# Two changes around an attention block's output projection: a written-out order for its tail, and the affine factors of the layer normalisation moved behind the transposition

## The chip, the cores and the metric

The kernel runs on one core of one Trainium2 chip. The metric is the device time of one execution in microseconds (us), shown as the median of three runs. TensorE (PE in the profile) multiplies matrices, VectorE (DVE), ScalarE (ACT) and GpSimd (POOL) do elementwise work, and SyncE (SP) issues the DMA transfers. Each engine works through its own queue of instructions in order and waits on semaphores for the others.

## The reference

The reference computes two layers of a decoder trunk for one sequence of 1024 tokens of width 1024, in float32. Layer 0 mixes tokens by dilated window attention, layer 1 by a gated linear recurrence (HGRN2). Each mixer is followed by a feed-forward block of width 4096 with a squared ReLU. Each of these four parts is added to its input and normalised:

```python
def layer_norm(x, g, b):
    xf = x.astype(F32)
    mu = jnp.mean(xf, axis=-1, keepdims=True)
    var = jnp.mean(jnp.square(xf - mu), axis=-1, keepdims=True)
    return ((xf - mu) * lax.rsqrt(var + LN_EPS) * g.astype(F32) + b.astype(F32)).astype(x.dtype)
...
for i in range(DEPTH):
    x = layer_norm(ALPHA * x + mixer(x), ln_mix_g[i], ln_mix_b[i])
    x = layer_norm(ALPHA * x + squared_relu_mlp(x, w_up[i], w_down[i]), ln_ffn_g[i], ln_ffn_b[i])
```

The loop is shortened. The affine factors g and b of a normalisation are vectors along the 1024 features.

The attention has three head groups with (window, dilation) = (128, 1), (512, 4) and (2048, 16). For each group it projects to q, k and v, rotates q and k by position (rotary embedding), computes softmax attention within the window, and at the end mixes the three groups' outputs per position and head, weighted by their softmax denominators. The mixed output, 1024 wide, is projected by W_out.

## The kernel before

**Precision.** Every matmul operand is split into a high and a low part (names end in h and l), and a product is three matmuls: high by high, low by high, high by low. The function `split` (L136 to L138) makes the parts: one instruction on ScalarE copies the high part (L137), one on VectorE subtracts it from the raw value (L138). In the large products the kernel uses Strassen's scheme with seven products for eight blocks, hence the many sums and differences of blocks (wc, wa, T1 to T4, S1 to S4).

**Stages.** By the trace: attention products and attention until 973 us, the projection by W_out with the last attention units until about 1118, the first feed-forward (up, then down) until about 1755, HGRN and its projection until 2250, the second feed-forward until the end.

**Attention.** `attention()` runs over `seq`, a list of product slots; in each slot TensorE computes one 512-wide product of twelve matmuls (L666 to L668). Three slots make the q, k and v of a unit of heads and a group. When the products of a unit are there, its attention is entered in a dictionary `fill` at slots given by tables: `ROPES` (rotary: `rope`, L465 to L474, four DMA issues that swap halves into a tile `rot`, a multiply by cos, L472, a multiply by sin, L473, an addition, L474), `OFFS` (the core: `qk` with the scores s, L500, the masked maximum, L511, the exponential, L514, `ptr` with the transposition ppt, L524, and `pv` with the output o, L539), `STATS` (the transposition mpt of the softmax statistics, L564) and `MIX` (the mix of the three groups: small [16, 128] instructions mn and ml, L592 to L605, the split of the weights into fh and fl, L609 and L611, six DMA issues that lay them out as rows, frow, L616, matmuls fb that spread them over the heads, L626, and the multiplications with the outputs og, L627 to L630). Steps due in a slot are issued behind its product.

TensorE and VectorE are kept in program order up to the last slot (`order`, an `in_order` block). Behind it a scheduler orders the instructions by its own costs and the program's priorities. The steps of the last two units, (7,1) and (7,0), and of the units whose slots lie past the end, come back from `attention()` as the list `lists`.

**Projection tail.** `outproj_ln()` (used for W_out of attention, `Out` with mixer 0, and of HGRN, mixer 1) computes z = ALPHA * x + o W_out by tiles of 128 tokens t and halves of 512 columns dm, over eight blocks k of 128 rows of W_out. For the attention k = 0 to 5 are ready first (`NKA`), so `stage_a` computes their part of some tiles, three tiles (0,0), (1,0), (2,0) together, then (0,1), (1,1), (2,1), (3,0), (3,1) one by one, and `tick()` issues the steps of `lists` between them, in equal shares of the ticks (a tick is three matmuls, L183 to L185). The z part is added by L933. Three blocks k (`PREA`) have their W_out and o split ahead, in the last slots of the attention. Behind the mix, `fin(t)` computes the rest of each tile, normalises it with `ln_math` and stores it to `x1d`; `tr(t)` transposes it (lnpt, L223) and splits it for the feed-forward (class `Fast`, which also keeps raw copies and forms the sums for Strassen's scheme, fs, L297 to L305).

**Layer normalisation.** `ln_math` (L193 to L214) does it in place on a [128, 1024] tile z:

```python
nc.vector.scalar_tensor_tensor(z, z, mv[:, 0:1], gB, op0=ALU.subtract, op1=ALU.mult)
...
act(z, z, AF.Copy, scale=w[:, 3:4])
nc.gpsimd.tensor_add(z, z, bB)
```

Statistics on VectorE (L196, L198), the subtraction of the mean and the multiplication with gB (g spread over the partitions) on VectorE (L199), the reciprocal root by Ln and Exp on ScalarE and a correction step on VectorE (L204 to L206), the scaling on ScalarE (L213), the addition of bB on GpSimd (L214). Only the last normalisation, with a store to the output, goes another way.

**Feed-forward.** `ffn()` computes up and down products in Strassen's scheme. In the down phase a function `after(n)` appends the closing work to a list `todo`, of which one entry is issued behind each step: residual loads, sums, `norm_of` (the normalisation and its store to `x3d`, L1296), `tr`/`ln_tr` (the transposition lnpt and the split of f0nh and f0nl, L233 and L234, directly out of the transposition's PSUM bank). No engine is kept in program order in the down phase. The loads of d (hidden activations, L1181) and their split d3s are on SP, ScalarE and VectorE next to that. The gates of HGRN begin directly behind.

Of the kernel before, what the change touches and what calls it, by code (L numbers as in the profile page):

```python
# [32 lines left out]
NSLOT = 50  # L33
NPRE = 2
PREA = 3
# [22 lines left out]
ROPES0 = ((-5, -2, -1, 2), (-4, 0, 1, 4))  # L58
# [4 lines left out]
def trunk_kernel(  # L63
# [15 lines left out]
    w_down: bass.AP,  # L79
    cos_t: bass.AP,  # L80
# [10 lines left out]
    wp = ctx.enter_context(tc.tile_pool(name="wp", bufs=3))  # L91
# [42 lines left out]
    nc.gpsimd.memset(one, 1.0)  # L134

# [57 lines left out]
    def ln_math(z, gB, bB, store=None):  # L193
# [5 lines left out]
        nc.vector.scalar_tensor_tensor(z, z, mv[:, 0:1], gB, op0=ALU.subtract, op1=ALU.mult)  # L199
        w = small([P, 4], "lnw")  # L200
# [6 lines left out]
        if store is not None:  # L207
            for i in range(2):
                c = slice(i * 512, i * 512 + 512)
                nc.vector.scalar_tensor_tensor(z[:, c], z[:, c], w[:, 3:4], bB[:, c], op0=ALU.mult, op1=ALU.add)  # L210
                nc.sync.dma_start(store[:, c], z[:, c])
            return
        act(z, z, AF.Copy, scale=w[:, 3:4])  # L213
        nc.gpsimd.tensor_add(z, z, bB)  # L214
# [21 lines left out]
    def ln_tr(t, z, xs):  # L236
        x_ = xs[t // 4]
        c = slice((t % 4) * P, (t % 4) * P + P)
        for j, pt in enumerate(z_tr(z)):
            put(x_.hi[2 * j:2 * j + 2], x_.lo[2 * j:2 * j + 2], pt, c)  # L240

    class Fast:


        def __init__(self, name):
            self.name, self.parts, self.raw, self.seen = name, {}, {}, []
# [18 lines left out]
        def add(self, t, z):  # L271
# [3 lines left out]
            v, g = nc.vector, nc.gpsimd  # L275
# [5 lines left out]
            def put_(n, src, eng=None):  # L281
                put(*self.tiles(n), src, c, eng)

            if half == 0:
                put_("11", p0)
                put_("21", p1)
            else:
                put_("22", p1)
            if first:
                a, b = ("11", "21") if half == 0 else ("12", "22")  # L290
                act(self.keep(a, t), p0, AF.Copy)
                act(self.keep(b, t), p1, AF.Copy)
                return
            t1, t2, t3, t4 = (scratch(n) for n in (1, 2, 3, 4))
            if half == 1:
                w12 = scratch(0)
                act(w12, p0, AF.Copy)  # L297
                v.tensor_sub(t3, p1, w12)
                g.tensor_sub(t1, w12, self.keep("11", t))
                put_("T3", t3)  # L300
                v.tensor_sub(t2, p1, t1)
                put_("T1", t1)
                g.tensor_sub(t4, self.keep("21", t), t2)
            else:
                b22 = self.keep("22", t)  # L305
                v.tensor_sub(t1, self.keep("12", t), p0)
                g.tensor_sub(t3, b22, self.keep("12", t))
                g.tensor_sub(t2, b22, t1)
                put_("T1", t1)
                v.tensor_sub(t4, p1, t2)  # L310
                put_("T3", t3)
# [10 lines left out]
    def attention(pre, hc):  # L322
# [124 lines left out]
        def constants():  # L447
            nc.sync.dma_start(cosT, cos_t)
            nc.sync.dma_start(sinT, sin_t)
            nc.sync.dma_start(mask, masks)  # L450

# [24 lines left out]
        def pieces(pr, g, qT, kT, vT, og, sS):  # L476
# [53 lines left out]
            def pv(b):  # L530
                if b % 4 == 0:
                    st["o"] = bank("o", "o")
# [19 lines left out]

            return [
# [152 lines left out]
        def unit_work(gi, a, base):  # L706
# [12 lines left out]
            def begin():  # L719
                ogs[pr][g] = U("og")  # L720
                p = pieces(pr, g, res.pop((a, 0)), res.pop((a, 1)), ep.pop((gi, 2, a)), ogs[pr][g], sS)
# [18 lines left out]
        order.__enter__()  # L740
        load_x("21", 0, (L, R))
# [19 lines left out]
        for n in range(len(seq)):  # L761
            gi, i, j = seq[n]
            load_w(n + LOADW)
# [12 lines left out]
            if n == len(seq) - 2 * PREA - 3:  # L776
                early = pre(oN)
            if n >= len(seq) - 2 * PREA - 1:
# [10 lines left out]
            if n % 21 == 14:  # L789
# [3 lines left out]
                for a in range(2):  # L793
# [14 lines left out]
                    for k, f in zip(MIX[a], mix):  # L808
                        at(base + k, f)
                if last:  # L810
                    for a in range(2):
                        for k, f in list(zip(ROPES0[a], tail[a][0])):
                            if k < -1:
# [4 lines left out]
        done = [f for n in sorted(fill) for f in fill[n]]  # L818
        mine = [[ra[0]], [rb[0], rb[1]], [ra[1]], [ca[0], rb[2]], [ca[1]], [cb[0]], [ca[2]], [cb[1]], [ca[3]], [cb[2]],
                [ca[4]] + sa, [cb[3]], [ca[5]], [cb[4]] + sb_, [cb[5]], mx[:1], mx[1:3], mx[3:5], [],  # L820
                mx[5:7], mx[7:10], mx[10:]]
        lists = [done[k:k + 1] + (mine[k] if k < len(mine) else []) for k in range(max(len(done), len(mine)))]
        return oN, lists


    class Out:
# [11 lines left out]
        def pre_steps(self, oN):  # L838
            for k in range(PREA):
                self.load(k, oN, 0)  # L840
                raw = U("wor")
                self.w[k] = (None, None, raw)
                nc.sync.dma_start(raw[:, :512], self.w_dram[k][:, :512])

            def steps():
                for k in range(PREA):
                    raw = self.w[k][2]
                    hi, lo = U("woh", F32R), U("wol", F32R)
                    self.w[k] = hi, lo, raw
                    split(raw[:, :512], hi[:, :512], lo[:, :512])  # L850
                    yield
                    self.split_k(k, 0)
                    yield

            return steps()
# [30 lines left out]
    def outproj_ln(pr, oN, fill, resid, gB_ap, bB_ap, keep):  # L886
# [864 lines left out]
```

## Time and profile before

| what | value |
| --- | --- |
| median of three runs | 2857.04 us (2854.59 to 2858.03) |
| the profiled execution's own time | 2856.82 us |
| its span, first to last instruction | 2854.6 us |
| mean granted TensorE clock | 0.995 |
| busy: TensorE, VectorE, ScalarE, GpSimd | 2789.4, 2053.8, 1448.4, 122.6 us |
| transfers | 485.25 MB, 170 GB/s |

A row of the profile names a line of the kernel, an engine, an operation and "out<-in" by the program's tile names without numbers. In a timeline the first two columns are start and duration in us. In the view of waits a row says which engine at which line waited for whom, then the total in us, how often, and the longest. Windows give, for a stretch of time, the busy time of each engine and the clock that was granted to TensorE (1.00 is full speed). A matmul of 512 columns is listed with 0.39 us, but the next one starts 0.227 us behind it; so the pace is read from starts, not from durations.

### The profile page before, as it was taken

To read this page: it belongs to the slowest core of one execution; us is meant where nothing else is said; L and a number is where in the kernel's file an instruction comes from. 1 tells how busy PE (TensorE), PEld (TensorE's weight loads), DVE (VectorE), ACT (ScalarE), POOL (GpSimd) and SP (SyncE) were. 2 spreads that over 40 slices of the span, in tenths; PEclk is the share of its full clock that TensorE was granted. 3 is DMA by queue.
4 is the path that set the end of the run, shared out by engine and by line. 5 is a ranking of instruction groups with operands and counts; after the bars stand their busy time and mean duration, and the time that the engine had idled before them with its cause. 6 is when DMAs were issued, how large, how long until landed. Compare 5 with 4: busy or idle time off the path is not lost.

```text
span 2854.6 us, 39893 instructions
## 1 busy us (share of the span) xinstructions
PE 2789.4 (98%) x14152; PEld 2235.3 (78%) x14152; DVE 2053.8 (72%) x3830; ACT 1448.4 (51%) x3105; POOL 122.6 (4%) x67
## 2 busy tenths in 40 slices
PE   8999999999999989999999999999999999999998
PEld 6777777777777767888878887778787788878887
DVE  7768777776887767786686875555667787678677
ACT  5555555655555555544454444554553645454433
POOL 0000000000000003000000011111102200000000
PEclk9999999999999999999999999999999999999999
DMA  7766665666667523464584843101131455475654
GB/s 291 249 201 193 190 197 171 215 206 204 198 198 222 154 77 133 156 220 156 173 303 126 275 142 104 38 30 60 51 120 71 159 202 174 155 268 189 223 176 132
DMA packets 204935, 485.25 MB, mean 170 GB/s; under 512 B 29376, under 2 KB 43712, under 8 KB 204736
## 3 DMA queue, kind: packets, MB, share of 16 engines
q1 hardware_dynamic: 204736, 482.72, 51.3%
q8 instruction: 111, 1.82, 0.3%
q14 instruction: 88, 0.72, 0.1%
HBM read 362.82 MB, written 94.24 MB: 160 GB/s over the span
## 4 chain that ended last, share of the span: by engine, by line
PE 90%; DVE 4%; ACT 2%; DMA 1%; issue 1%; POOL 0%; SPq 0%; DVEq 0%; POOLq 0%; ACTq 0%
PE pmm L666 8%; PE pmm L668 8%; PE pmm L667 8%; PE pup L1114 7%; PE pup L1112 7%; PE pup L1113 7%; PE pdy L1264 4%; PE pdy L1260 4%; PE pdy L1263 4%; PE pmm L171 3%; PE s L500 3%; PE pdx L1263 3%; PE pdx L1264 3%; PE pdx L1260 3%; PE pmm L173 3%; PE pmm L172 3%
## 5 line engine op out<-in xcount | busy, mean ns | idle before, releaser
L666 PE MATMUL pmm<-xh,H 128*128 128x512 f32 x1008 | 407.7, 404 | 12.0 <-ACT H L432 8.5
L668 PE MATMUL pmm<-xh,H 128*128 128x512 f32 x1008 | 396.4, 393 | 0.0
L667 PE MATMUL pmm<-xl,H 128*128 128x512 f32 x1008 | 396.1, 393 | 0.0
L666 PEld LDWEIGHTS pmm<-xh,H 128*128 128x128 f32 x1008 | 191.2, 190 | 52.3 <-ACT H L432 8.5
L668 PEld LDWEIGHTS pmm<-xh,H 128*128 128x128 f32 x1008 | 190.4, 189 | 41.9 <-DVE H L440 0.3
L667 PEld LDWEIGHTS pmm<-xl,H 128*128 128x128 f32 x1008 | 191.1, 190 | 36.9
L514 ACT ACTIVATE p<-p,stats 128x128 f32<-128x128 f32 (+1 forms) x384 | 168.3, 441 | 92.6 <-DVE stats L511 92.2
L1263 PE MATMUL pdy<-dT,dS 128*128 128x512 f32 x512 | 199.2, 389 | 0.0
L1260 PE MATMUL pdy<-dT,dS 128*128 128x512 f32 x512 | 199.2, 389 | 0.0
L1264 PE MATMUL pdy<-dT,dS 128*128 128x512 f32 x512 | 199.2, 389 | 0.0
L511 DVE CUSTOM_DVE_ANT_0 p<-s,mask 128x128 f32<-128x128 f32 (+1 forms) x384 | 113.2, 347 | 68.4 <-PE s L500 58.8
L137 ACT ACTIVATE dS<-dr 128x512 fp32r<-128x512 f32 x192 | 119.5, 622 | 73.3 <-PE pdy L1264 36.6
L171 PE MATMUL pmm<-f0nh,wh 128*128 128x512 f32 x384 | 153.1, 399 | 0.0
L173 PE MATMUL pmm<-f0nh,wl 128*128 128x512 f32 x384 | 149.8, 390 | 0.0
L172 PE MATMUL pmm<-f0nl,wh 128*128 128x512 f32 x384 | 149.6, 390 | 0.0
L138 DVE TENSOR_TENSOR dS<-dr,dS 128x512 fp32r<-128x512 f32 x192 | 135.1, 703 | 16.5 <-ACT dS L137 16.5
L214 POOL TENSOR_TENSOR z<-z,bB 128x1024 f32<-128x1024 f32 x24 | 58.5, 2442 | 1687.8 <-ACT z L213 1678.3
L527 ACT ACTIVATE pts<-ppt 128x256 f32<-128x256 f32 (+1 forms) x192 | 85.3, 474 | 62.7 <-PE ppt L524 60.5
L137 ACT ACTIVATE dT<-hold 128x512 fp32r<-128x512 f32 x128 | 80.0, 625 | 69.5 <-DVE hold L1239 28.8
L1073 ACT ACTIVATE H<-wc 128x512 fp32r<-128x512 f32 x128 | 77.2, 625 | 74.6 <-DVE wc L1066 43.9
L1263 PEld LDWEIGHTS pdy<-dT,dS 128*128 128x128 f32 x512 | 96.1, 188 | 20.0
L1264 PEld LDWEIGHTS pdy<-dT,dS 128*128 128x128 f32 x512 | 96.1, 188 | 20.0
(395 smaller groups left out, 6927.9 us busy)
## 6 DMA issues: line engine op xcount, KB each, us to landing
xh<-xtd SPq DMA_DIRECT2D x110, 512.0 KB
xl<-xtd SPq DMA_DIRECT2D x110, 512.0 KB
dr<-hd SPq DMA_DIRECT2D x192, 256.0 KB
dr<-in_w_down_dram SPq DMA_DIRECT2D x128, 256.0 KB
rot<-e SPq DMA_DIRECT2D x192, 128.0 KB
wa<-in_w_up_dram SPq DMA_DIRECT2D x48, 512.0 KB
wb<-in_w_attn_dram SPq DMA_DIRECT2D x36, 512.0 KB
wa<-in_w_attn_dram SPq DMA_DIRECT2D x33, 512.0 KB
```

The source lines that it names most:

```text
L171: nc.tensor.matmul(o, wh[:, k], xs.h(k), start=k == 0, stop=False)
L172: nc.tensor.matmul(o, wh[:, k], xs.l(k), start=False, stop=False)
L173: nc.tensor.matmul(o, wl[:, k], xs.h(k), start=False, stop=k == NK - 1)
L666: nc.tensor.matmul(o, wh, hi[k // 2][:, c], start=begin and k == 0, stop=False, skip_group_check=True)
L667: nc.tensor.matmul(o, wh, lo[k // 2][:, c], start=False, stop=False, skip_group_check=True)
L668: nc.tensor.matmul(o, wl, hi[k // 2][:, c], start=False, stop=end and k == 3, skip_group_check=True)
L1112: nc.tensor.matmul(o, wh, xf.h(b, k), start=begin and k == 0, stop=False, skip_group_check=True)
L1113: nc.tensor.matmul(o, wh, xf.l(b, k), start=False, stop=False, skip_group_check=True)
L1114: nc.tensor.matmul(o, wl, xf.h(b, k), start=False, stop=end and k == 3, skip_group_check=True)
L1260: nc.tensor.matmul(o[q], h, T_[:, L], start=begin, stop=False, skip_group_check=True)
L1263: nc.tensor.matmul(o[q], h, T_[:, R], start=False, stop=False, skip_group_check=True)
L1264: nc.tensor.matmul(o[q], l, T_[:, L], start=False, stop=end, skip_group_check=True)
```

## The change

It has two parts.

**A fixed order in the tail of the attention.** The core of the last two units is now split in six steps of another grouping and placed at ticks (`TCORE`); statistics and mix get ticks of their own (`TSTATS`, `TMIX`), and so do the loads and splits of the blocks k. `stage_a` takes one tile half at a time: (0,0), (1,0), (2,0), (0,1), (1,1), (2,1) with six k, then (3,0), (3,1), (4,0), (4,1) with seven. TensorE and VectorE stay in program order through the tail, and SP from slot 228 on. Six blocks k instead of three are split ahead during the last slots. The mix of the units before the last ones comes at earlier slots (`MIX0`), and the order of `fin` behind the mix differs.

**Affine factors behind the transposition.** `ln_unit` only normalises: VectorE makes scale and bias [128, 1], and one ScalarE instruction applies both. g and b are applied per feature behind the transposition, where the features lie on the partitions: `gained` issues four ScalarE instructions of 128 columns for each transposed bank, into an SBUF tile, and the split reads that tile. Where z itself is needed further with its factors (the residual of the feed-forward, and `x3d`), VectorE multiplies by and adds a spread copy of g and b: `gain` and `bias` in the feed-forward, `final` for `x3d`, the latter issued during HGRN's start as `late` steps. The differences of class `Fast` that were on GpSimd move to VectorE.

```diff
-NSLOT = 50
+NSLOT = 49
-PREA = 3
+PREA = 6
+PINSP = 228
+MIX0 = (20, 21, 21, 22, 23, 25, 26, 27, 27, 28, 29, 30, 30, 31)
-ROPES0 = ((-5, -2, -1, 2), (-4, 0, 1, 4))
+ROPES0 = ((-5, -2, -2, 0), (-4, -1, -1, 0))
+TCORE = ((3, 9, 15, 21, 27, 33), (6, 12, 18, 24, 30, 36))
+TROPE = (1, 5)
+TSTATS = ((25, 26, 30), (28, 29, 33))
+TMIX = (38, 40, 41, 43, 44, 48, 49, 50, 51, 52, 53, 54, 55, 55)
...
-    wp = ctx.enter_context(tc.tile_pool(name="wp", bufs=3))
+    wp = ctx.enter_context(tc.tile_pool(name="wp", bufs=4))
...
+    def ln_unit(z):
+        mv = ln_scale(z)
+        w = ln_rsqrt(mv)
+        nc.vector.tensor_scalar(w[:, 4:5], mv[:, 0:1], w[:, 3:4], -1.0, op0=ALU.mult, op1=ALU.mult)
+        act(z, z, AF.Identity, scale=w[:, 3:4], bias=w[:, 4:5])
...
+    def gained(pt, j, col, dst):
+
+        for i in range(4):
+            k = j * 4 + i
+            c = slice(i * P, i * P + P)
+            act(dst[:, c], pt[:, c], AF.Identity, scale=lc[:, col, 0, k:k + 1], bias=lc[:, col, 1, k:k + 1])
+        return dst
...
         for j, pt in enumerate(z_tr(z)):
-            put(x_.hi[2 * j:2 * j + 2], x_.lo[2 * j:2 * j + 2], pt, c)
+            raw = gained(pt, j, col, wp.tile([P, 512], F32, name="lnr", tag="p" if j else "pts"))
+            put(x_.hi[2 * j:2 * j + 2], x_.lo[2 * j:2 * j + 2], raw, c)
...
-                    st["o"] = bank("o", "o")
+                    st["o"] = bank("mm" if last == 2 else "o", "o")
...
+            if last:
+                return [
+                    [lambda: qk(0), vtrans],
+                    [lambda: ptr(0), lambda: ptr(1), lambda: qk(2)],
+                    [lambda: pv(0), lambda: pv(1), lambda: ptr(2), lambda: ptr(3), lambda: qk(4)],
+                    [lambda: pv(2), lambda: pv(3), lambda: ptr(4), lambda: ptr(5), lambda: qk(6)],
+                    [lambda: pv(4), lambda: pv(5), lambda: ptr(6), lambda: ptr(7)],
+                    [lambda: pv(6), lambda: pv(7)],
+                ]
...
+            if n == PINSP:
+                queue.__enter__()
...
-        order.__exit__()
...
+        on(TROPE, (ra[0], rb[0]))
+        for a, (core, stats) in enumerate(((ca, sa), (cb, sb_))):
+            on(TCORE[a], core)
+            on(TSTATS[a], stats)
+        on(TMIX, mx)
+        return oN, events, (order, queue)
...
+        def tail():
+            def on(t, f):
+                fill.setdefault(t, []).append(f)
+
+            for n, k in enumerate((6, 7)):
+                on(4 + 6 * n, lambda k=k: pr.load_raw(k))
+                for dm in range(2):
+                    on(26 + 12 * n + 2 * dm, lambda k=k, dm=dm: pr.split_raw(k, dm))
+            for k in range(6):
+                on(4 * k, lambda k=k: pr.load(k, oN, 1))
+                on(19 + 3 * k, lambda k=k: split_k(k, 1))
+            for n, k in enumerate((6, 7)):
+                on(32 + 24 * n, lambda k=k: (pr.load(k, oN, 0), split_k(k, 0)))
+                on(34 + 23 * n, lambda k=k: split_k(k, 1))
+            for t, dm in [(0, 0), (1, 0), (2, 0), (0, 1), (1, 1), (2, 1), (3, 0), (3, 1), (4, 0), (4, 1)]:
+                load_z(max(t, 1) + 1)
+                stage_a([(t, dm)], list(range(6 if t < 3 else 7)))
+            assert not fill, sorted(fill)
+            for o in orders:
+                o.__exit__()
...
-                ln_math(z[t], gB, bB)
+                ln_unit(z[t])
                 nc.sync.dma_start(keep[t * P:(t + 1) * P, :], z[t])
...
+        def gain(t):
+            v.tensor_mul(z[t], z[t], norm["rg"])
+
+        def bias(t):
+            v.tensor_add(z[t], z[t], norm["rb"])
...
+        def final(t):
+            v.tensor_mul(z[t], z[t], norm["g"])
+            v.tensor_add(z[t], z[t], norm["b"])
+            nc.sync.dma_start(x3d[t * P:(t + 1) * P, :], z[t])
...
-            ln_math(z[t], norm["g"], norm["b"])
-            nc.sync.dma_start(x3d[t * P:(t + 1) * P, :], z[t])
+            ln_unit(z[t])
...
-        return xn, []
+        return xn, [] if last else [lambda t=t: final(t) for t in (4, 5, 6, 7, 0, 1, 2, 3)]
```

More of the change, by code (lines that the diff above doesn't have):

```diff
@@ L918, in tick @@
         def tick():
+            if orders:
+                for f in fill.pop(count[0], []):
+                    f()
+                count[0] += 1
+                return
             count[0] += 1
```

231 lines of the change are left out of this document (134 added, 97 removed).

## The prediction

> **What bounds the kernel now.** I read the page first (busy times, the chain that ended last), then the windows by stage, then TensorE's waits in the two stages that the change touches, then the timelines around the longest of them.
>
> ```profile
> span 2854.6 us, 39893 instructions
> PE 2789.4 (98%) x14152; PEld 2235.3 (78%) x14152; DVE 2053.8 (72%) x3830; ACT 1448.4 (51%) x3105; POOL 122.6 (4%) x67
> PE 90%; DVE 4%; ACT 2%; DMA 1%; issue 1%; POOL 0%; SPq 0%; DVEq 0%; POOLq 0%; ACTq 0%
> ```
>
> TensorE is the bound. The change leaves its work as it is (the built programs hold the same matmuls), so the time can move only by its waits and by the clock granted to it. The windows show both.
>
> ```profile
> 973.00:1043.00 70.00, 66.47 (x415) 1.00 0.27 78
> 1048.00:1052.00 4.00, 4.00 (x11) 0.57 0.00 0
> 1058.00:1069.00 11.00, 10.38 (x23) 0.53 0.40 131
> 1741.00:1745.00 4.00, 4.00 (x14) 0.57 0.87 346
> 1700.00:1755.00 55.00, 48.90 (x225) 38.65 (x225) 40.49 (x90) 32.00 (x77) 8.00 (x4) 0.97 0.27 89
> ```
>
> After the stretch come its length, busy times (in the first four TensorE alone; in the last PE, PEld, DVE, ACT, POOL), the granted clock, DMA share and GB/s. The half-clock stretches cost 4 x (1 - 0.57) = 1.7 us, 11 x (1 - 0.53) = 5.2 us and 1.7 us. The waits, for the projection tail (973 to 1118 us) and then for the end of the first feed-forward (1700 to 1830 us):
>
> ```profile
> PE pmm L183 <- ACT aoh L137: 4.0, 2, 3.6
> PE fb L626 <- DMA frow<-fh: 1.9, 1, 1.9
> PE pmm L183 <- DVE z L933: 1.3, 1, 1.3
> PE pmm L183 <- DVE vT L701: 0.8, 1, 0.8
> PE o L539 <- ACT og L550: 0.7, 2, 0.4
> PE s L500 <- DVE kT L474: 0.5, 1, 0.5
> ...
> PE lnpt L223 <- POOL z L214: 3.2, 3, 1.5
> PE pdx L1260 <- ACT d3s L137: 2.3, 1, 2.3
> PE lnpt L223 <- DVE f0nl L234: 1.5, 3, 0.7
> ```
>
> So the tail holds 4.0 + 1.9 + 1.3 + 0.8 + 0.7 + 0.5 = 9.2 us of waits and 1.7 + 5.2 = 6.9 us of lost clock: **16.1 us** that another order could take back. The end of the feed-forward holds 3.2 + 2.3 + 1.5 + 1.7 = **8.7 us**. These two sums are the most that I see the change win there.
>
> **Part 1, the order of the tail.** It now is written out by ticks of three matmuls. Attention for the last two units starts with `qk(0)` at tick 3, behind twelve projection matmuls. In the built program TensorE's order there is 3 projection matmuls, `o`, `ppt`, `mpt`, 9 projection matmuls, `s`: fixed, so if `s` is not ready, nothing behind it runs. `s` needs the rotated kT, the last of a series on VectorE, also fixed. The durations of its members are in these timelines of TensorE and VectorE (start, duration).
>
> ```profile
> 969.51 0.71 PE L500 MATMUL s<-kT,qT 64*128 64x128 f32 x8
> ...
> 973.19 0.39 PE L668 MATMUL pmm<-xh,H 128*128 128x512 f32 x1
> ...
> 971.11 2.35 DVE L473 TENSOR_TENSOR rot<-rot,sinT 128x1024 f32<-128x1024 f32 x2
> 973.38 2.05 DVE L474 TENSOR_TENSOR qT<-qT,rot 128x1024 f32<-128x1024 f32 x1
> 975.33 1.03 DVE L701 TENSOR_TENSOR vT<-pmm,vp 128x512 f32<-128x512 f32 x1
> 976.20 0.35 DVE L592 TENSOR_TENSOR mn<-ml 16x128 f32<-16x128 f32 x1
> 976.47 0.67 DVE L138 TENSOR_TENSOR wol<-wor,woh 128x512 fp32r<-128x512 f32 x1
> 977.08 0.40 DVE L593 TENSOR_TENSOR mn<-mn,ml 16x128 f32<-16x128 f32 x1
> ...
> 978.01 0.88 DVE L595 TENSOR_TENSOR ml<-mn,ml 16x128 f32<-16x128 f32 x3
> ...
> 979.40 1.21 DVE L474 TENSOR_TENSOR qT<-qT,rot 128x1024 f32<-128x1024 f32 x1
> 980.54 0.54 DVE L598 TENSOR_TENSOR ml<-ml 16x384 f32<-16x384 f32 x1
> ...
> 983.65 0.94 DVE L603 RECIPROCAL mn<-mn 16x128 f32<-16x128 f32 x1
> ```
>
> The series in the new order, from the same place in it (971.1 us, after the four maxima behind the `s` at 969.51): rot 1.17 (half of the x2), qT 1.95 (start to start), kT in the same strided form 1.95, wol 0.6, vT 0.9, two mn 0.75, three ml 0.8, rot 1.17, qT and kT of the other unit 1.14 each (as the qT at 979.40), ml 0.5, two mn 0.75, the reciprocal 0.95, three ml 0.8, rot 1.17, kT 1.95. That is 17.7 us, so kT is there at 988.8. The last product's matmul starts at 973.2, and TensorE gets to `s` after twelve matmuls of 0.23 (2.7 us), `o` (0.6), `ppt` and `mpt` (0.6): near 977.6. **A new wait of 11 us** in front of the 64 ticks. Its ends: 8 if the strided qT and kT ran at the plain 1.2 us instead of 2.0, 13 if the loads of rot or the exponentials in between add to the series. Before, projection matmuls that need no `s` ran in that time; now all of them queue behind it. While it stands, VectorE, ScalarE and the queues catch up, so I expect the small waits of 9.2 us to go, except those behind the last mix.
>
> The second place is `fb` of the last mix. Its first step is placed at tick 38, `fb` at tick 48: thirty matmuls.
>
> ```profile
> 1044.81 0.36 DVE L592 TENSOR_TENSOR mn<-ml 16x128 f32<-16x128 f32 x1
> ...
> 1051.87 0.63 SPq L616 DMA_DIRECT2D frow<-fh  x1
> ...
> 1055.63 0.61 SPq L616 DMA_DIRECT2D frow<-fl  x1
> ...
> 1053.00 0.39 PE L183 MATMUL pmm<-woh,aoh 128*128 128x512 f32 x1
> ...
> 1055.49 0.39 PE L185 MATMUL pmm<-woh,aol 128*128 128x512 f32 x1
> 1057.75 0.70 PE L626 MATMUL fb<-frow,bsel 128*128 128x512 f32 x2 [1.87 <-DMA frow<-fh]
> ```
>
> From mn to fb took 12.9 us: 7 on VectorE and ScalarE, then six DMA issues in a row and their landing. Four 0.6 us instructions of others stood in it; in the new order three do, so 12.3. Thirty matmuls at (1055.49 - 1053.00) / 11 = 0.227 us cover 6.8. **A new wait of 5.5 us** (3 to 7). Each of the two waits is longer than the one of 3.58 us (the 3.6 above) that was followed by the 4 us at 0.57: I add 1.7 us for the first, and for the second 3.4, between this 1.7 and the 5.2 behind the `fb` of 1057.75.
>
> A rule speaks against the change here: the Trainium skill, "TensorE: Matmul & The Clock Gate", Part 1, says that the clock falls to half after an idle window of some 3.4 us and returns after a busy one. By it both waits would cost one window at half, 1.7 us, and the sum for part 1 would be 1.7 us lower. The trace agrees for the 3.58 us wait, not for the 1.87 us one, which was followed by 11 us at 0.53.
>
> Sum of part 1: -16.1 + 11 + 5.5 + 1.7 + 3.4 = **+5.5 us**, from -1 to +10 by the ends. Six instead of three splits of W_out now lie in the last 22 product slots (twelve more pieces, each some 0.6 us on VectorE and on ScalarE): hidden, as VectorE had 22 us idle in the 93 us before the tail.
>
> ```profile
> 880.00:973.00 93.00, 91.75 (x549) 71.92 (x548) 70.55 (x153) 53.50 (x151) 0.00 (x0) 1.00 0.66 205
> ```
>
> **Part 2, the affine factors.** Each of 24 normalisations loses the 1024-wide multiply with gB on VectorE and the addition of bB on GpSimd, and gains one [128,1] instruction.
>
> ```profile
> L199 DVE SCALAR_TENSOR_TENSOR z<-z,lnmv,gB x32: 1267/1285/3411, 1070.4 to 2847.8; 128x1024 f32<-128x1024 f32 x32
> L214 POOL TENSOR_TENSOR z<-z,bB x24: 2357/2396/3154, 1074.5 to 2231.1; 128x1024 f32<-128x1024 f32 x24
> L233 ACT ACTIVATE f0nh<-lnpt x32: 361/383/386, 1699.7 to 1765.2; 128x256 fp32r<-128x256 f32 x32
> ```
>
> Its chain is 1.3 + 2.4 - 0.2 = 3.5 us shorter. The 3.2 us of waits for POOL go, being three of at most 1.5. Against that, two times four ScalarE instructions of 128 columns now stand between a transposition and the split. None such is in the trace: not over the 0.38 us of the 256-column one and not under half of it, so 0.8 to 1.5 us for four; I take 1.2. They, and no longer f0nl, now free the transposition's bank; of f0nl's 1.5 us of waits I leave half, as the nearest I can say between none and all. Inside the stages this is some -1.5 us (from -3 to +3) for both starts of the feed-forward and the second projection, whose waits were small.
>
> The factors come back as 1024-wide instructions on VectorE at the 1.17 us of rot: 16 for the residual in each feed-forward (19 us, hidden if VectorE, 72% busy over the span, takes them in its gaps), and 16 for `x3d`: 2.3 us for each tile. In the new order five of these pairs lie between the last low halves of d3s and f0nl, that is in the stretch 1700 to 1755, where VectorE had 14.5 us free. The chain there gives back 4 x 1.2 = 4.8 and takes 11.7: it fits, with 7 left, but a d3s or f0nl behind a pair comes up to 2.3 us later. The d3s wait of 2.3 came from SP: the load of d stood behind `x3d` stores that waited for POOL's z.
>
> ```profile
> 1731.94 2.68 SPq L1296 DMA_DIRECT2D x3d<-z  x2
> ```
>
> In the new order loads of d still stand behind such stores, now waiting for VectorE. I count POOL's 3.2, half of f0nl's 1.5, the 2.3 and 1.7 less 2 us for one pair: **-6 us**, from -8.7 to +6 (five pairs, each in front of something that TensorE needs, would add 11.7, and half a clock stretch).
>
> **Sum.** +5.5 - 6 - 1.5 = -2 us. The profiled execution took 2856.8 us (span 2854.6 and 2.2 around it), the median is 0.2 above: 2854.8, rounded to **2855**.
>
> **The rivals.**
> *The early wait isn't there.* If kT is ready by 978, the tail gives back 16.1 less 5.5 and 3.4: -7, with -7.5 from part 2 that is 2842; with the whole 8.7, 2839. For it: VectorE was busy for only 70.55 of the 93 us before the tail, so less of the mix could be left over. Against: the series above starts behind an `s` that TensorE itself issues at 969.5, and its members are counted.
> *Slower: the pairs for x3d.* One mechanism in one place: VectorE's order at the end of the first feed-forward puts 2.3 us pairs ahead of low halves, and TensorE stands for each, with a stretch at half clock. It decides from the third pair on: three cost 7 us and 1.7, which is all that part 2 takes back; five cost 11.7 and 1.7, then part 2 is +4.7 - 1.5 and the kernel 2865. With the long ends of part 1 (+10), 2870.
> *The shorter chain isn't on the path* (the change doesn't do what it says): the 3.2 us for POOL turn into waits for ScalarE's eight instructions at the same transposition. Then part 2 is -2 and the time 2859; I count it with the forecast.
>
> **How the numbers follow.** Forecast 2855, own range 2847 to 2864: 0.42. Early wait absent, about 2841: 0.28. Slower, about 2867: 0.30. A measurement tells 0.2%, 5.7 us, from no change: faster is below 2851.3, slower above 2862.7. Of the forecast's 0.42 I put 0.10 below, 0.27 within, 0.05 above; of the slower case 0.02 within. Faster 0.38, same 0.29, slower 0.33. The range 2836 to 2874 takes in the ends of both other cases but for their tails.
>
> **What would show it.** An `s` after the first twelve projection matmuls that waits 8 to 13 us for VectorE's kT, and half a clock behind it; an `fb` that waits 3 to 7 us for frow; no wait of lnpt for POOL; a d3s that waits less than 2.3 us. The forecast is wrong if `s` waits under 4 us, or if waits for f0nl and d3s between 1700 and 1770 sum to over 6 us.

## The result, and the profile after

The changed kernel takes 2879.53 us (median, 2877.04 to 2882.68) against 2857.31 us: 1.0076 times as long, 95% interval 1.0065 to 1.0087. It is **22 us slower**, where no change was forecast (2855, range 2836 to 2874). Both medians are of six executions; the profiled one of the changed kernel took 2882.68 us and was the longest of its six, so that the stages below add up to 26 us where the medians differ by 22.

The head of its page, and from the views of single tiles when the first and the last matmul of a stage started (the numbers behind "x": shortest, median and longest ns of one, then first and last start in us). First the changed kernel:

```profile
span 2880.9 us, 40061 instructions
PE 2794.6 (97%) x14152; PEld 2242.4 (78%) x14152; DVE 2065.1 (72%) x3896; ACT 1503.6 (52%) x3273; POOL 41.7 (1%) x27
...
L191 PE MATMUL pmm<-woh,aoh x128: 387/389/774, 980.5 to 1123.3; 128*128 128x512 f32 x128
L1203 PE MATMUL pup<-af11h,H x64: 389/389/795, 1124.0 to 1426.5; 128*128 128x512 f32 x64
L1618 PE MATMUL as<-qe,ls x128: 275/275/579, 1823.3 to 2141.8; 128*128 128x128 f32 x128
```

Then the same tiles of the kernel before:

```profile
L183 PE MATMUL pmm<-woh,aoh x128: 387/389/796, 973.4 to 1117.7; 128*128 128x512 f32 x128
L1112 PE MATMUL pup<-af11h,H x64: 388/389/496, 1118.3 to 1414.1; 128*128 128x512 f32 x64
L1508 PE MATMUL as<-qe,ls x128: 274/275/580, 1803.2 to 2120.4; 128*128 128x128 f32 x128
```

TensorE does as many matmuls as before (x14152 in both pages), in 26.3 us more of span. The start times cut the span into stages: the projection tail (from the first wo matmul to the first `pup`), up 1 (to the first `pdx`), down 1 with HGRN's start (to the first `as`), HGRN (to the second projection), projection 2, up 2, down 2. Lengths in us:

| kernel | until the tail | tail | up 1 | down 1, HGRN's start | HGRN | projection 2 | up 2 | down 2 |
| --- | --- | --- | --- | --- | --- | --- | --- | --- |
| before | 973.4 | 144.9 | 313.3 | 371.5 | 317.2 | 105.4 | 313.2 | 315.6 |
| after | 980.5 | 143.5 | 320.1 | 379.2 | 318.5 | 103.4 | 320.3 | 315.4 |

So the 26 us are 7.1 before the tail, 6.8 and 7.1 in the two starts of the feed-forward, 7.7 at the end of the first, and 1.3 in HGRN; the tail, where the forecast had 5.5 us more, is 1.4 shorter, and the second projection 2.0. TensorE's waits in the changed kernel, from 973 to 1130, 1118 to 1700 and 1700 to 1850 us:

```profile
PE s L525 <- DVE kT L499: 11.3, 1, 11.3
PE fb L660 <- DMA frow<-fl: 2.8, 1, 2.8
PE ppt L549 <- ACT pts L552: 0.9, 1, 0.9
...
PE pup L1203 <- ACT H L1164: 2.8, 2, 1.7
PE lnpt L249 <- ACT fs L239: 2.1, 1, 2.1
PE pup L1203 <- ACT upa L1208: 1.4, 1, 1.4
...
PE as L1618 <- DVE qe L1754: 4.7, 1, 4.7
PE lnpt L249 <- ACT lnr L239: 3.7, 3, 1.4
PE pdx L1351 <- ACT d3s L145: 2.6, 1, 2.6
PE pdx L1351 <- ACT dT L145: 1.6, 1, 1.6
PE pdx L1355 <- DVE d3s L146: 1.4, 2, 0.8
PE lnpt L249 <- ACT z L223: 1.0, 1, 1.0
```

L239 is the new line `gained`, four instructions of 128 columns. It stands in front of `lnpt` at both places, and the matmuls `pup` wait for other work of ScalarE. What ScalarE does there, at the start of up 1, and TensorE beside it:

```profile
1139.35 0.46 ACT L239 ACTIVATE fs<-lnpt,lncol 128x128 f32<-128x128 f32 x1 [0.82 <-PE lnpt L249]
1139.71 0.40 ACT L259 ACTIVATE afT1h<-fs 128x256 fp32r<-128x256 f32 x1
1140.02 0.45 ACT L239 ACTIVATE fs<-lnpt,lncol 128x128 f32<-128x128 f32 x1
1140.36 0.41 ACT L259 ACTIVATE afT2h<-fs 128x256 fp32r<-128x256 f32 x1
...
1142.61 0.47 ACT L239 ACTIVATE fs<-lnpt,lncol 128x128 f32<-128x128 f32 x1
1142.95 1.16 ACT L1164 ACTIVATE H<-wa 128x512 fp32r<-128x512 f32 x2
...
1138.71 1.03 PE L249 MATMUL lnpt<-ident,z 128*128 128x128 f32 x8
1141.82 0.66 PE L249 MATMUL lnpt<-ident,z 128*128 128x128 f32 x4 [2.07 <-ACT fs L239]
1144.16 0.80 PE L1203 MATMUL pup<-af11h,H 128*128 128x512 f32 x1 [1.69 <-ACT H L1164]
```

ScalarE works without a gap from 1139.35 on: the small instructions of one tile lie between the splits (afT1h, afT2h) of the tile before, so a bank is held for 2 us and more, the next transposition waits 2.07, and H, which `pup` needs, comes last. Behind the wait of `s` (first row, TensorE alone) and behind these waits (second row) the granted clock is at half:

```profile
996.50:1002.50 6.00, 5.99 (x23) 0.50 0.17 50
1144.00:1149.00 5.00, 4.83 (x11) 3.80 (x12) 4.76 (x10) 3.55 (x10) 0.00 (x0) 0.50 0.00 0
```

At the end of the first feed-forward ScalarE works without a gap from 1746.88 to 1761.79. The three longest waits of TensorE for ScalarE in this stretch, all behind L239 there, are of `lnpt` at 1748.41 (1.42) and 1750.42 (1.35) and of `pdx` at 1760.29, whose d3s stands behind sixteen instructions of L239 in the last 8.3 us:

```profile
1757.73 1.60 ACT L239 ACTIVATE lnr<-lnpt,lncol 128x128 f32<-128x128 f32 x4
...
1759.71 1.14 ACT L145 ACTIVATE d3s<-d 128x256 fp32r<-128x256 f32 x3
...
1760.29 0.64 PE L1351 MATMUL pdx<-dT,d3s 128*128 128x512 f32 x1 [2.60 <-ACT d3s L145]
```

Whether the load of that d had landed earlier, the profile doesn't show. Waits are only part of the loss. Windows of TensorE over down 1 with HGRN's start, before and after, and three stretches in the latter:

```profile
1431.70:1803.20 371.50, 358.00 (x1594) 0.99 0.54 180
1444.10:1823.30 379.20, 363.04 (x1594) 0.98 0.54 180
1719.50:1723.00 3.50, 3.50 (x11) 0.51 1.04 363
1750.50:1753.50 3.00, 3.00 (x10) 0.50 1.01 284
1760.50:1767.50 7.00, 6.49 (x16) 0.51 0.67 226
```

Of the 7.7 us more, 2.7 are idle time (16.2 for 13.5) and 5.0 longer busy time for the same 1594 matmuls. The three stretches at half clock cost half of their 13 busy us, 6.4; before, one of 4 us cost 1.7.

### The profile page after: what moved, and what is told of

It is laid out like the page before. It is cut to its first block, busy times and chain, and to the rows that moved or that the text cites. A ratio compares the mean times of both kernels' runs of the same rounds, so it can differ in the third digit from the quotient of the medians.

```text
span 2880.9 us, 40061 instructions
## 1 busy us (share of the span) xinstructions
PE 2794.6 (97%) x14152; PEld 2242.4 (78%) x14152; DVE 2065.1 (72%) x3896; ACT 1503.6 (52%) x3273; POOL 41.7 (1%) x27
## 5 line engine op out<-in xcount | busy, mean ns | idle before, releaser
L1354 PEld LDWEIGHTS pdy<-dT,dS 128*128 128x128 f32 x512 | 96.1, 188 | 20.1
L1351 PEld LDWEIGHTS pdy<-dT,dS 128*128 128x128 f32 x512 | 96.1, 188 | 19.9
L1355 PEld LDWEIGHTS pdy<-dT,dS 128*128 128x128 f32 x512 | 96.1, 188 | 19.8
```

The lines of the kernel that those rows point to most:

```text
L1351: nc.tensor.matmul(o[q], h, T_[:, L], start=begin, stop=False, skip_group_check=True)
L1354: nc.tensor.matmul(o[q], h, T_[:, R], start=False, stop=False, skip_group_check=True)
L1355: nc.tensor.matmul(o[q], l, T_[:, L], start=False, stop=end, skip_group_check=True)
```

## The experiments

Theory at their start: the tail's order costs what was forecast for it, and the affine factors cost some 20 us, by the four small ScalarE instructions. Rivals: the parts act on each other; the detour through SBUF or the factors given back on VectorE are the price. Each ratio is to the kernel before on the same chip, with its 95% interval. A difference to the changed kernel is one of medians from different rounds; the intervals of e4, e5, e6, e7 and e10 overlap with that of the changed kernel (1.0065 to 1.0087), so for these the lengths of the stages say more than the 5 to 7 us.

**e1: the tail's order alone** (the normalisation of before put back).

> The changed kernel with the layer normalisation of before (its gB and bB inside the chain, GpSimd's addition and differences), so the order of the tail alone, with the changed pools. Theory (the two parts add up; in the traces the tail costs 5.6 us of TensorE's time, 4.8 in the last slots before it and 0.8 in it; the rest, some 20 us, is the affine part): 2863, from 2859 to 2867, with the wait of s for kT at 11 us. Rival (the parts act on each other: the tail's order sends the feed-forward into a worse state): 2857 or less, or above 2870.

2862.19 us, 1.0015 (1.0006 to 1.0025). **e2: the affine factors alone** (attention and tail of before, the changed pools).

> The changed kernel with the tail of before (three blocks split ahead, free order behind the last slot), so the affine factors alone, with the changed pools. Theory (the parts add up): 2874 to 2879, with waits of lnpt for the four ScalarE instructions behind the transposition and half a clock behind them. Rival (they act on each other): below 2868.

2874.38 us, 1.0054 (1.0039 to 1.0069). Both are as their theories had it, and the parts add up: +4.3 and +16.5 us are 20.8 of 22. So part 1 is near its forecast of +5.5, and part 2 is the miss (-7.5 forecast).

**e3: one copy.**

```diff
-        for i in range(4):
...
-            act(dst[:, c], pt[:, c], AF.Identity, scale=lc[:, col, 0, k:k + 1], bias=lc[:, col, 1, k:k + 1])
+        act(dst, pt, AF.Copy)
```

> The changed kernel with one ScalarE copy of 512 columns in place of the four instructions with factor and bias, so g and b are left out in what the feed-forwards and HGRN read. Theory (the four instructions are the price: 1.4 us for each bank against 0.6, in front of what TensorE waits for): 2862 to 2868. Rival (the detour through SBUF with its later split, or the factors given back on VectorE, are the price, whatever the copy costs): above 2873.

2854.56 us, 0.9986 (0.9976 to 0.9995): 25 us below the changed kernel, more than expected, and the detour through SBUF and the factors given back on VectorE stay in it. **e4: nothing given back on VectorE** (`final` without its arithmetic, and the steps `gain` and `bias` taken out).

> The changed kernel without the multiplications and additions on VectorE that give the factors back to z, so g and b are left out in the residual of the feed-forwards and in x3d. Theory (four ScalarE instructions are the price): 2874 to 2880, hardly less than the changed kernel's 2879.5. Rival of the prediction (pairs for x3d in front of low halves at the end of the first feed-forward): 2871 or less, with the waits between 1700 and 1860 us gone.

2873.80 us, 1.0055 (1.0039 to 1.0072), 5.7 below, just under the theory's range. 5.2 of it are at the end of the first feed-forward. Both matter; the four instructions matter most. Stages of these four:

| kernel | until the tail | tail | up 1 | down 1, HGRN's start | HGRN | projection 2 | up 2 |
| --- | --- | --- | --- | --- | --- | --- | --- |
| e1 tail only | 980.8 | 144.7 | 312.7 | 371.0 | 318.6 | 105.4 | 312.8 |
| e2 affine only | 974.3 | 141.4 | 319.2 | 379.2 | 318.5 | 103.3 | 318.7 |
| e3 one copy | 983.5 | 141.5 | 312.1 | 367.2 | 317.5 | 103.3 | 312.1 |
| e4 no give-back | 980.7 | 142.8 | 319.3 | 374.0 | 317.5 | 103.4 | 319.2 |

With one copy each of the three places is better than before (312.1, 367.2, 312.1 against 313.3, 371.5, 313.2): with the second projection it is 8.7 us, near the gain of 7.5 that had been forecast for part 2, and the four instructions eat it and more. At the end of the first feed-forward e3 has none of the three stretches at half clock, and idles 9.8 us:

```profile
1437.10:1804.30 367.20, 357.42 (x1594) 1.00 0.56 185
```

Of the 12.0 us to the changed kernel, 6.4 are idle time and 5.6 busy time. Is it ScalarE's time? **e5** puts them on VectorE (`nc.vector.tensor_scalar` with multiply and add), **e6** two on each engine.

> The changed kernel with the four instructions behind the transposition on VectorE (multiply and add with two [128,1] operands, 128 columns each) in place of ScalarE. Theory (ScalarE's 1.4 us for each bank stand in front of what TensorE waits for, and ScalarE's queue is the one that is short there): 2858 to 2866, the waits of lnpt and pup for ScalarE gone. Rival (any engine's four instructions of 128 columns cost as much, and VectorE was 79% busy at these places): 2872 or more, with waits for VectorE instead.

> The changed kernel with two of the four instructions on ScalarE and two on VectorE. Theory (the price grows with ScalarE's time for a bank: 0.5 us with one copy gave 2854.6, 1.4 us gave 2879.5): near 2861, from 2856 to 2868. Rival (it is the order that the scheduler gives ScalarE, not the time): 2872 or more, or no relation to the time.

2874.08 (1.0067, 1.0049 to 1.0085) and 2873.95 us (1.0061, 1.0045 to 1.0077): some 5.5 us better each, far above both theories' numbers and within the rivals' (2872 or more). ScalarE's time as such is not the price; it costs on VectorE too (up 1, down 1 and up 2 at 317.7, 375.1 and 318.5 in e5). The views of the tile `lncol`, in the changed kernel and e5, the one copy's row in e3, and e9's, below:

```profile
L239 ACT ACTIVATE fs<-lnpt,lncol x64: 442/466/502, 1133.0 to 2289.2; 128x128 f32<-128x128 f32 x64
```

```profile
L239 DVE TENSOR_SCALAR fs<-lnpt,lncol x64: 398/403/413, 1128.3 to 2280.2; 128x128 f32<-128x128 f32 x64
```

```profile
L236 ACT ACTIVATE fs<-lnpt x16: 588/595/604, 1133.9 to 2261.5; 128x512 f32<-128x512 f32 x16
```

```profile
L240 POOL TENSOR_SCALAR lnr<-lnr,lncol x64: 439/618/2408, 1713.2 to 1810.7; 128x128 f32<-128x128 f32 x64
```

128 columns take 0.47 us on ScalarE and 0.40 on VectorE, 512 columns 0.60: four small instructions are, by their lengths, 2.7 to 3.1 times the one. Is it the bank that they hold? **e9** copies once on ScalarE and applies the factors in SBUF on GpSimd, **e10** the same on VectorE.

```diff
+        act(dst, pt, AF.Copy)
         for i in range(4):
...
-            act(dst[:, c], pt[:, c], AF.Identity, scale=lc[:, col, 0, k:k + 1], bias=lc[:, col, 1, k:k + 1])
+            nc.gpsimd.tensor_scalar(dst[:, c], dst[:, c], ...)     # e10: nc.vector
```

> The changed kernel with one ScalarE copy of 512 columns out of the transposition's bank, and the factors put on in SBUF behind it by four GpSimd instructions. Theory (what TensorE waits for is the bank: four instructions of 0.46 us hold it for 1.4 us and more, a copy for 0.6): 2856 to 2864, near the one copy's 2854.6. Rival (the whole way from the transposition to the split counts, with four fixed costs on whatever engine): 2872 or more.

> The same with the four instructions in SBUF on VectorE in place of GpSimd. Theory (the bank is what counts): 2858 to 2866, below the 2874.1 with VectorE reading the bank itself. Rival (fixed costs on an engine that is needed there): 2872 or more.

e9: 2902.08 us, 1.0157 (1.0142 to 1.0172), much slower; GpSimd's instructions reach 2.4 us, and down 1 with HGRN's start takes 395.5 us. e10: 2872.67 us, 1.0055 (1.0040 to 1.0070), with up 1 and up 2 at 315.1 each, 5 us less than the changed kernel, but down 1 with HGRN's start at 378.9, no less. So the theory holds in part at the starts of the feed-forward, where `lnpt` waited for the bank (5 of the 8 us that one copy gives there), and falls at the end of the first one. **e11** gives the late transpositions more room (`LATE` 3 for 2).

> The changed kernel with three product steps instead of two between the late transpositions at the start of both feed-forwards (16 steps for four tiles, the last just ahead of its use). Theory (four small instructions for each bank make a queue because the tiles come close together): some 4 to 8 us of the 10 that the two starts lose more come back, 2871 to 2876. Rival (the order within one tile is the price, however far the tiles are apart): 2878 or more; or slower, if the last tile now comes too late for the product that reads it.

2898.07 us, 1.0143 (1.0126 to 1.0160): slower, up 1 328.9 us. The last tile comes too late, as the rival allowed:

```profile
PE pup L1203 <- ACT afT2h L259: 6.1, 1, 6.1
PE lnpt L249 <- ACT fs L239: 4.2, 1, 4.2
```

The queue of small instructions isn't cured by that. **e13** asks what the give-back for `x3d` costs: its work or its place. `final` is ordered behind the last instruction that VectorE has been given, and starts six products later.

> The changed kernel with the eight pairs for x3d ordered on VectorE behind the last low half of f0nl, in HGRN's first products. Theory (where the pairs stand costs 6 us: they hold VectorE for 2.4 us each, and it waits in front of them for the transposition that reads z): 2871 to 2875, the stretch 1700 to 1860 losing 22 to 24 us of TensorE's time instead of 29. Rival (their work costs, wherever it stands): 2878 or more, the loss moved into HGRN's start.

2879.84 us, 1.0077 (1.0062 to 1.0092): nothing gained. Down 1 with HGRN's start falls to 374.0 as in e4, but HGRN takes 322.7 instead of 318.5, with a new wait of 3.2 us of its transpositions for VectorE. The pairs for `x3d` are what costs 5.2 us there, as e13 keeps `gain` and `bias`; moved, they cost 4.2 in HGRN. It is the work, in both places that were tried.

**The tail.** **e7** starts the core at tick 12 instead of 3 and puts the mix of the unit before behind kT. **e12**, on e1, has the same later core, but puts that mix three slots earlier than the changed kernel (`MIX0` from 17 to 28). Of the edit of e7:

```diff
-TCORE = ((3, 9, 15, 21, 27, 33), (6, 12, 18, 24, 30, 36))
+TCORE = ((12, 17, 22, 27, 32, 37), (15, 20, 25, 30, 35, 40))
...
```

> The changed kernel with the attention core of the last units begun nine ticks later (first at tick 12, steps of five ticks), the mix of the unit before two slots later, behind kT, and the last mix at ticks 41 to 61. Theory (the 11.3 us in front of s are VectorE's series up to kT, 17.8 us, of which the mix is 5): kT some 5 us earlier and s 6 us later, so the wait under 2 us and the kernel 9 to 13 us below the changed one, 2867 to 2871. Rival (kT comes later too, as the loads of rot or the splits end last): the wait stays above 6 us, the kernel above 2873.

> The normalisation of before, and the fixed tail with the core nine ticks later as in the run with the core later, but with the mix of the unit before three slots earlier than in the changed kernel, ahead of the last rotations. Theory (in the run with the core later, s waited 6.1 us for maxima that stood behind half of that mix; put ahead, into VectorE's idle time before 969 us, it costs nothing): no wait over 3 us for s, 2848 to 2853, faster than before. Rival (VectorE is full in the last slots, so the mix only moves the wait to kT): 2855 to 2862.

e7: 2873.03 us, 1.0062 (1.0046 to 1.0078), 6.5 below the changed kernel, less than expected, with the tail at 135.5 for 143.5. The time is the rival's, but not for its reason: kT no longer makes `s` wait, but the second pair of `s` waits for maxima behind the mix:

```profile
1001.17 1.99 PE L525 MATMUL s<-kT,qT 64*128 64x128 f32 x8 [6.13 <-DVE stats L536]
```

e12: 2854.43 us, 0.9991 (0.9981 to 1.0000), 7.8 below e1 and at most a little faster than before; the tail is 137.4 us for 144.7. It missed its range (2848 to 2853) by 1.4. Until the tail it still takes 978.2. That loss has a wait of 2.7 us of `o` in it; in the changed kernel the granted clock is at half behind it, from 948 to 952. The rows of ScalarE and TensorE in the changed kernel:

```profile
944.18 0.60 ACT L731 ACTIVATE e<-pmm 128x512 f32<-128x512 f32 x1 [2.12 <-PE pmm L702]
...
946.19 0.60 ACT L572 ACTIVATE og<-o 128x512 f32<-128x512 f32 x1
...
946.84 1.09 PE L564 MATMUL o<-pts,vn 128*64 128x128 f32 x16 [2.70 <-ACT og L572]
```

ScalarE stood idle for a later product with the copy of og queued behind it, though the matmuls `o` that it copies had ended at 936.6. **e8** keeps ScalarE in program order there, **e14** puts only the earlier mix into the kernel before, and **e17** (on e15) leaves SP to the scheduler.

> The changed kernel with ScalarE, like SP, in program order from slot 228 through the tail. Theory (the 4.8 us lost in the last slots, an o that waits 2.7 us for og, come from the scheduler putting the copy of og behind evacuations of later products): that wait gone, 2874 to 2877. Rival (it is the splits of W_out, six for three, that fill ScalarE): no change within 2 us, or slower.

> The kernel before with only the mix of the unit before the last ones at the changed kernel's earlier slots. If the earlier mix costs the 4.8 us in the last slots (an o that waits 2.7 us for og): 2859 to 2863 with that wait between 940 and 950 us. If the six early splits do: 2854 to 2858 without it.

> The fastest kernel so far (core and mix moved, normalisation without GpSimd) with SP left to the scheduler instead of program order. If SP's order costs the 4.8 us in the last slots: the o that waits 2.7 us for og gone, 2843 to 2846. If the six early splits do: that wait stays, and the time is 2847 to 2852, or more where the tail's loads now come late.

e8: 2884.01 us, 1.0098 (1.0082 to 1.0114), slower: that wait goes, but others of 3.1 and, in the tail, 11.6 us for ScalarE take its place. e14: 2859.09 us, 1.0004 (0.9994 to 1.0013), without the wait; its time just falls into the range of the first reading, but the wait isn't there and the tail begins at 973.1. e17: 2846.07 us, 0.9959 (0.9945 to 0.9973), between the two ranges, with the wait. The kernels with three early splits reach the tail at 973.1 to 974.3 us, those with six at 978.2 to 983.5. So neither the earlier mix, SP's order nor the ticks are the cause by themselves, and fixing ScalarE's order is no cure; what is left are the six splits, with their loads, or the changed slots of the last rotations. These two were not tried apart.

**A shorter chain without the four instructions.** One VectorE instruction takes the place of ScalarE's scaling and GpSimd's addition: **e15** on e12, **e18** on the kernel before.

```diff
-        act(z, z, AF.Copy, scale=w[:, 3:4])
-        nc.gpsimd.tensor_add(z, z, bB)
+        nc.vector.scalar_tensor_tensor(z, z, w[:, 3:4], bB, op0=ALU.mult, op1=ALU.add)
```

> The run with core and mix moved (normalisation of before) and in the normalisation one VectorE instruction, z times the reciprocal root plus bB, in place of ScalarE's scaling and GpSimd's addition. Theory (the chain is 2.3 us shorter without anything behind the transposition): the waits of lnpt for z, 3.7 us, go, 2848 to 2852, faster than both kernels. Rival (VectorE is what is short there): 2854 or more.

> The kernel before with only the one VectorE instruction in place of ScalarE's scaling and GpSimd's addition. Theory (its gain, 6 us in the traces at the end of the first feed-forward and 2 at the start of the second, doesn't depend on the tail): 2849 to 2853. Rival (it needs the other tail): 2855 or more.

e15: 2848.62 us, 0.9969 (0.9957 to 0.9980). e18: 2846.19 us, 0.9961 (0.9946 to 0.9976), better than expected. Both beat both kernels; e15 has no wait of `lnpt` for z and none of `pdx` for d3s. e18's waits from 1700 to 1860 us:

```profile
PE as L1507 <- DVE qe L1643: 4.7, 1, 4.7
PE pdx L1259 <- ACT d3s L137: 2.6, 1, 2.6
PE lnpt L222 <- DVE f0nl L233: 1.3, 2, 0.7
PE pdx L1259 <- ACT dT L137: 0.5, 1, 0.5
```

The wait for POOL is gone. **e16** puts all remedies into the changed kernel (ticks and mix of e12, copy of e10, place of e13).

> The changed kernel with all that helped: core later and mix earlier, one ScalarE copy out of the bank with the factors put on in SBUF by VectorE, the pairs for x3d behind the low halves. Theory (the gains add: 7.8 for the tail, 6.8 for the copy, 6 for the pairs): 2857 to 2862, no better than the kernel before. Rival (with VectorE freed of the pairs, the copy gives as much as the one copy alone did): 2853 or less.

2862.80 us, 1.0019 (1.0009 to 1.0029): 0.8 above the theory's range. Against e12, which has the same tail and the normalisation of before, the affine part still costs some 8 us.

| kernel | until the tail | tail | up 1 | down 1, HGRN's start | HGRN | projection 2 | up 2 |
| --- | --- | --- | --- | --- | --- | --- | --- |
| e15 | 981.8 | 137.9 | 314.1 | 364.3 | 318.2 | 103.3 | 312.9 |
| e16 | 980.4 | 136.4 | 315.8 | 371.0 | 322.9 | 103.3 | 315.8 |
| e18 | 973.6 | 142.5 | 313.1 | 368.4 | 318.2 | 103.3 | 312.7 |

## Why the prediction was wrong, point by point

- **The wait of `s`: right.** Forecast 11 us, measured 11.3. The series on VectorE was forecast at 17.7 us; it ran from 978.57 to 996.46, 17.9. These are its end and what it released:

```profile
994.56 1.90 DVE L499 TENSOR_TENSOR kT<-kT,rot 128x1024 f32<-128x1024 f32 x1
...
996.51 1.66 PE L525 MATMUL s<-kT,qT 64*128 64x128 f32 x8 [11.35 <-DVE kT L499]
```

- **The wait of `fb`: half its size.** The chain took the forecast 12.3 us, but its cover was 9.5 us instead of 6.8, so the wait was 2.8 instead of 5.5:

```profile
1050.90 0.37 DVE L626 TENSOR_TENSOR mn<-ml 16x128 f32<-16x128 f32 x1
...
1063.21 0.47 PE L660 MATMUL fb<-frow,bsel 128*128 128x512 f32 x1 [2.84 <-DMA frow<-fl]
```

  A tick fixes a place in TensorE's order, not a time on VectorE: mn was placed at tick 38 and began behind the z of tick 36, as soon as VectorE was free. I had counted the cover from its tick. The half clock was booked with 1.7 us behind the first wait and 3.4 behind the second; it cost 3.0 (6 us at 0.50) and 1.7 (4 us at 0.57, from 1064 on).
- **"Hidden, as VectorE had 22 us idle": wrong.** Until the tail the changed kernel takes 7.1 us more. Spare time of one engine over 93 us says nothing about the order in the queue of another; that the early splits do it is what the exclusions leave, not shown by itself.
- **"The time can move only by its waits and by the clock granted to it": not so in the tail.** With the same 694 matmuls TensorE is idle 6.1 us more than before, but busy 7.5 us less, of which the clock explains only some 2; why the rest ran closer together is open.

```profile
973.40:1118.30 144.90, 134.83 (x694) 0.95 0.30 100
980.50:1124.00 143.50, 127.29 (x694) 0.94 0.26 90
```

  The loss before the tail on one side, the smaller `fb` wait and this on the other nearly cancel: +4.3 for part 1, forecast +5.5, is the right sum by luck.
- **Part 2, the step that failed:** "two times four ScalarE instructions of 128 columns now stand between a transposition and the split", priced at "0.8 to 1.5 us for four; I take 1.2", and then booked beside the path ("some -1.5 us"; of f0nl's waits "I leave half"). The size for four was about right: started 0.35 us apart they take 1.4 us. The bound under it was not: "not over the 0.38 us of the 256-column one" measured 0.47. The Trainium skill, "ScalarE: Activation LUTs", What ACT_TABLE_LOAD costs, states 186 ns and 0.833 ns for each column, and some 93 ns more for each [128,1] operand; for 128 columns and two operands that is an estimate of 479 ns. The trace agrees, with 466 ns.
- What was wrong is the place. By e2 the affine part alone costs 5.9 and 5.5 us in the two starts of the feed-forward and 7.7 at the end of the first, where -1.5 (with the second projection) and -6 had been booked. At the starts of the feed-forward each of these four stands in front of the next transposition and of H, so a gain turned into +6.8 and +7.1 us, half clock included; one copy in their place gives -1.2 and -1.1 against before. At the end of the first feed-forward they cost 12 us (379.2 against 367.2). There, e5, e6 and e10 show that another engine or an earlier release of the bank does not bring the 12 us back. Six of the 12 are half clock, a cost that the forecast had as falling to nothing there (it counted the 1.7 of before as won). In the changed kernel three of the four longest waits stand behind L239 on ScalarE; in e10 they are of `lnpt` for z (4.1) and of d3s for VectorE (3.9). So the work turns into waits on whichever engine has it; which order of the queues would hide it was not tried.
- **The rival of the pairs for `x3d`: half right.** They cost 5.2 us at its place (e4, e13), where the forecast had 2 and the rival, from three pairs on, 8.7 and more; two waits for low halves of d3s, 1.4 us in all, go without them, and so does half of the lost clock. But another order gains nothing (e13).
- **That the 3.2 us of waits for POOL go: right,** and they are worth more: e18 takes 10.5 us off with that one line, by the lengths of its stages 3.1 us where these waits stood and 4.5 in the tail and the second projection. In the changed kernel waits of `lnpt` for L239 came in their place (3.7), as the rival "the shorter chain isn't on the path" had it; it put part 2 at -2 where it was +16.5.
- **The d3s wait of 2.3, counted as won: wrong.** It was put down to `x3d` stores that waited for POOL's z. It is 2.6 in the changed kernel and 2.6 in e18, where POOL has no part in the normalisation.
- **The signs.** Waits for f0nl and d3s over 6 us were to show the forecast wrong; there were 4.0 for d3s and none for f0nl, although it was wrong. The loss lay in `lnpt` and in the clock, which the sign left out.

## What to carry to other kernels

An instruction is priced by where it stands: four short ones between a transposition and the next use of its bank were 1.4 us for each bank, and 12 us for a stage, although ScalarE was busy for only 52% of the span. About half of the 12 was the half clock behind the waits, which a sum of waits doesn't show. When work moves from one wide instruction to several narrow ones, first look up what the narrow one costs at its own width with its own operands; a wider one without them in the trace is no upper bound. If a chain is to be shortened, try the smallest edit that takes the slow member out before moving its arithmetic: one line gave 10.5 us where the rearrangement lost 16.5.

## What the runs showed of the hardware

- A ScalarE instruction of 128x128 from PSUM with a factor and a bias for each partition took 0.47 us, a copy of 128x512 0.60. On VectorE the small one took 0.40 from PSUM and, in e10, 0.34 from SBUF.
- On GpSimd, in SBUF, the small one took 0.44 to 2.4 us (e9, median 0.62 at the end of the first feed-forward); e9 took 22.5 us longer than the changed kernel.
- Behind the wait of 11.35 us the granted clock was 0.50 for 6 us. Shorter waits were followed by half clock too: 0.50 from 1144 to 1149 behind waits of 2.07 and 1.69 us that lay closely together, and 0.51 from 1760.5 to 1767.5 behind one of 2.60, with one of 0.52 in it.
